# One encoder block on one core: bias rows copied with the repetitions outermost, and kept results loaded later in the down projection

## The chip, the cores and the metric

The kernel runs on 1 core of one Trainium2 chip, with every tensor in float32. The metric is the device time of one execution in microseconds (us), lower is better; several executions give a median.

## What is computed

One layer of a hybrid block over 512 positions of 1024 channels. The reference, cut to what matters here:

```python
def reference(...):
    h = _layernorm(x, ln_in_g, ln_in_b)
    mix = _mixing(h, ...)                      # SSD branch and attention branch, gated, one output projection
    h = _layernorm(DN_ALPHA * h + mix, ln1_g, ln1_b)
    f = _conv_ffn(h, ffn_w_up, ffn_conv_w, ffn_conv_b, ffn_w_down)
    return _layernorm(DN_ALPHA * h + f, ln2_g, ln2_b)

# attention, per block of 128 queries:
    logits = jnp.einsum('bthc,btkc->bthk', ql, kv)
    bias = jnp.take(rel_bias, _t5_bucket(idx - qpos[None, :, None]), axis=0)   # 16 heads, by key minus query
    logits = logits + bias.transpose(0, 1, 3, 2)

def _conv_ffn(h, w_up, conv_w, conv_b, w_down):
    u = _causal_dwconv(h @ w_up, conv_w, conv_b)
    a, v = jnp.split(u, 2, axis=-1)
    return (jax.nn.silu(a) * v) @ w_down       # w_down is 2816 x 1024
```

## The kernel before

**Products.** Each float32 operand is split into a high part (ACT copies it, L178 or L192) and a low part (DVE subtracts, L179 or L193), and TensorE (PE) adds three products, high by high, high by low and low by high, at L254. So every weight block passes through a DMA into `wraw` (issued by SyncE, SP), an ACT copy into `whi` and a DVE subtraction into `wlo` before PE may use it. There are four `wraw` buffers and three pairs `whi`, `wlo`. PE's order is fixed by hand (`chain`), and it runs through the program almost without a pause.

**The SSD stage** (to about 440 us) projects one block after another for four groups `g`. `in_x`, `in_b` and `in_c` end in a convolution (`conv_silu`: ACT at L649, three DVE steps at L652, ACT at L654, DVE at L655), `in_z` in a gate (ACT L688, DVE L689). `ssd_d` leaves two results in PSUM, which DVE (L813) and then POOL (L814, L824) turn into `v`, and ACT squares `v` (L830). `out_br` projects the results of the group before; for the first group ACT moves its sums from PSUM to `mssd` (L702), and only then is that PSUM buffer (`pacc`, three of them) free for the next projection. ACT, DVE and POOL each work strictly in their own order.

**The bias rows.** The bias depends on key minus query only, so each head has one row of 384 numbers (`UW`) in `rb_d`. `t5_copy(q)` writes 128 copies (`P`) of the rows of four heads into `rs_d`, from DRAM to DRAM, 768 KB in one DMA on SP's queue; it is called four times, q = 0 to 3, at fixed places of the SSD stage for groups 1 and 2. The attention stage reads `rs_d` with a row step of UW - 1 into one tile `toe` per head (L1017), which gives each query its shifted row.

**The up projection and what it keeps.** The down projection multiplies sums and differences of blocks, and takes pairs of up results (operands `fX`, made in `operands`). Six of the up results go to DRAM as `fo_d`, and one combination of each pair as `q_d` (`spill`, L1273, on POOL's queue). In the down projection (`NC` = 11 steps `c`, each 24 products long), they come back by `loaded` (L1537) into the tiles `f0` to `f5` and `f10` to `f14`, 256 KB each. `late(c + 4, ...)`, called for c = 4, 5 and 6, uses `f0` to `f5`; `q_split`, from c = 5 on, uses `f10` to `f14`. The weights of step c come by `w_sums(c)`: a half from `w_dq` and `sd_d` (L1491, L1492) and a second 512 KB from `sd_d` (L1493), into `raw` or `wraw`; in the lists below `raw_9797` and `raw_9798` are the two parts of c = 0.

**What sets the order.** `w_sums` issues at a high priority and each `loaded` behind the weight load written last (`issue_after(last_w)`), so SP's list is a mixture of both in the order in which the scheduler met them. SP's DMAs share one queue with at most eight in flight: each waits until the one eight places before it is done, and whatever SP waits for holds all that is behind it. ACT and DVE steps of the down projection are ordered by due times (`plan`).

Of the kernel before, what the change touches and what calls it, by code (L numbers as in the profile page):

```python
# [16 lines left out]
P = 128  # L17
# [14 lines left out]
UW = 384  # L32
# [42 lines left out]
def block_kernel(ctx, tc, A, out):  # L75
    nc = tc.nc
# [15 lines left out]
    def wt(tag, shape, name, dtype=F32):  # L92
        return wk.tile(shape, dtype, name=name, tag=tag, bufs=BUFS[tag])
# [18 lines left out]
    def acc_tile():  # L112
        return ps("acc", 3)
# [6 lines left out]
    def any_tile(tags):  # L120
        rot[0] += 1
        return ps(tags[rot[0] % len(tags)])
# [84 lines left out]
    def w_(name, s, **kw):  # L207
        return wload(A[name][s], **kw)
# [115 lines left out]
    rb_d = dram.tile([AH, UW], F32, name="rb_d")  # L324
    rs_d = dram.tile([AH, P, UW], F32, name="rs_d")
# [5 lines left out]
    fo_d = dram.tile([6, P, T], F32, name="fo_d")  # L331
# [178 lines left out]
    for j in range(2, 4):  # L510
        p = any_tile("abc")
# [367 lines left out]
    def t5_copy(q):  # L879

        n = AH // 4
        with tc.issue_after(last_w[0].ins):
            nc.sync.dma_start(rs_d[q * n:(q + 1) * n], bass.AP(tensor=rb_d.tensor, offset=rb_d.offset + q * n * UW,
                                                               ap=[[UW, n], [0, P], [1, UW]]))

    decays()
    latents()
# [51 lines left out]
    for g in (1, 2):  # L939
        run([in_x(g, 3), in_z(g, 0), in_z(g, 1), in_b(g + 1), out_br(g - 1, 0), out_br(g - 1, 1), out_br(g - 1, 2)],  # L940
            pair(g, 0, AT, root=AT[0], gm=(26, 29),
                 more=[(45, pin), *([(18, t5_load), (46, t5_rows)] if g == 1 else [(30, t5_copy, 2)])]))
        run([in_x(g + 1, 0), in_z(g, 2), in_c(g + 1), in_x(g + 1, 1), in_z(g, 3), out_br(g - 1, 3),
             in_x(g + 1, 2)], pair(g, 2, AT, [(12, ssd_b, g + 1), (38, ssd_cb, g + 1), *([(42, pin), (30, t5_copy, 3)] if g == 2 else [(12, t5_copy, 0), (44, t5_copy, 1)])]))
# [224 lines left out]
    for n in range(KD):  # L1169
        w, p = merges[n] if n < len(merges) else (w_("w_br_att", n), None)  # L1170
# [3 lines left out]
        p, first = (p, NP - 1) if p else (acc_tile(), 0)  # L1174
# [77 lines left out]
    def f_tile(c, dtype):  # L1252
        return fp.tile([P, T], dtype, name=f"f{c}", tag=f"f{c}")
# [181 lines left out]
    for s in range(3, 2 * KF + 1):  # L1435
# [16 lines left out]
        elif s < 2 * KF:  # L1452
            p = acc_tile() if s % 2 else any_tile("abc")
# [19 lines left out]
    def step(p, x_, i, w, first, last):  # L1473

        for j, (a, b) in enumerate(((0, 0), (1, 0), (0, 1))):
            mm(p, x_[a][:, tok(i)], w[b], start=first and j == 0, stop=last and j == 2)
# [6 lines left out]
    def w_sums(c, k0, k1):  # L1483

        with tc.high_priority(offset=400):
            if c % 4 < 2 and c < NC - 1:
                r = [wt("g4" if c % 4 else "k4", [P, D], "raw") for _ in range(2)]
            else:
                r = [wrw.tile([P, D], F32, name="wraw", tag="wraw") for _ in range(2)]
            with tc.issue_after(mark.ins):  # L1490
                nc.sync.dma_start(r[0][:, :T], A["w_dq"][c][:, 0])  # L1491
                nc.sync.dma_start(r[0][:, T:], sd_d[c][:, 0])  # L1492
                last_w[0] = nc.sync.dma_start(r[1].rearrange("p (a b) -> p a b", a=2), sd_d[c][:, 1:3])  # L1493
            if c % 3:
                d = [room[c % 3 - 1][:2], room[c % 3 - 1][2:]]
            else:
                d = [whl_pair() for _ in range(2)]
            for (hi, lo), src, k in zip(d, r, (k0, k1)):
                parts(k, k + 1.2, hi, lo, src)
        b11, t1, t3, t2 = [(hi[:, half_of(h)], lo[:, half_of(h)]) for hi, lo in d for h in range(2)]  # L1500
        return {"A11": b11, "S1": t1, "S3": t3, "S2": t2}
# [19 lines left out]
    lc, fO, fQ = [0], {}, {}  # L1521
# [11 lines left out]
    def loaded(c, src):  # L1533

        t = f_tile(c, F32)
        with tc.issue_after(last_w[0].ins):
            nc.sync.dma_start(t, src)  # L1537
        return t

    def late(c, k):  # L1540

        r0, r1 = fO[2 * c - 16], fO[2 * c - 15]
        s = wt("v", [P, T], "s")
        b, a = [(l_tile(), l_tile()) for _ in range(2)]
        z = l_tile()
        tt(k, s[:, L_], r0[:, R_], r1[:, R_], OP.subtract)
        tt(k, s[:, R_], s[:, L_], r0[:, L_], OP.subtract)
        tt(k, r0[:, R_], r0[:, L_], r0[:, R_], OP.subtract)
        parts(k + 1, k + 1.9, *b, s)
        parts(k + 1.6, k + 2.6, *a, r0)  # L1550
        parts(k + 2.2, k + 3.3, z[:, L_], z[:, R_], r1[:, R_])
        tt(k + 3.3, r1[:, R_], r1[:, L_], s[:, R_], OP.add)
        fX.append({"A11": [t[:, L_] for t in a], "S3": [t[:, R_] for t in a], "S1": [t[:, L_] for t in b],
                   "S2": [t[:, R_] for t in b], "A22": [z[:, L_], z[:, R_]]})
        fQ[c] = r1
# [7 lines left out]
    def q_split(c, k):  # L1563
        x_ = l_tile(), l_tile()
        parts(k, k + 0.8, *x_, fQ[c])
        qs.append(x_)
# [8 lines left out]
    def w_next():  # L1575
        n = wn[0]
        wn[0] += 1
        part = halves_[2 * n:2 * n + 2]
        srcs = [sd_d[c][:, 3] if kind == "X4" else A["w_dq"][c][:, 3 if kind == "B21" else 2] for kind, c in part]
        k = early.get(n, tB + use[n] * STEP - 6)  # L1580
        for key, w in zip(part, w_pair(srcs, k, cyc[n % 7])):
            wB[key] = w

    for c in range(NC):
        t = c * PAIR
        k0, k1 = {0: (-9.5, -4.6), 1: (0.2, 1.4), 2: (3.2, 4.6)}.get(c, (t - 5.5, t - 4.3))
        w = w_sums(c, k0, k1)
        if c in (1, 2):
            for j in range(3):
                fO[3 * c + j - 3] = loaded(3 * c + j - 3, fo_d[3 * c + j - 3])  # L1590
        for q, j in {1: ((0, 10), (1, 11)), 2: ((2, 12), (3, 13), (4, 14)), 6: ((5, 0), (6, 2)), 7: ((7, 4),)}.get(c, ()):
            fQ[q] = loaded(j, q_d[q])
        if c in (4, 5, 6):
            late(c + 4, t - 3)
        for q in {5: (0, 1), 6: (2, 3), 7: (4, 5), 8: (6, 7), 9: (8, 9)}.get(c, ()):
            q_split(q, t + 0.5 + 2.2 * (q % 2))
        if c == NC - 1:
            h1 = [wt("k4" if i < 2 else "g4", [P, D], "h1") for i in range(NT)]
            for i in range(NT):
                nc.sync.dma_start(h1[i], h1_d[:, i])  # L1600
            for _ in range(4):
                w_next()
        prods = [(U, "A11"), (P6, "S2"), (P7, "S3"), (P5, "S1")]
        for p, x_ in prods if c else (prods[0], prods[3], prods[2], prods[1]):
            for i in range(2):
                step(p[i], fX[c][x_], i, w[x_], c == 0, c == NC - 1)
# [104 lines left out]
    n = T // 2  # L1711
# [99 lines left out]
```

## Time and profile before

| | us |
|---|---|
| median of 3 runs | 1080.3 |
| lowest and highest run | 1078.89, 1081.57 |
| the profiled execution | 1078.5 |
| its span, first to last instruction | 1076.8 |
| PE busy | 1060.1 |
| DVE busy | 873.5 |
| ACT busy | 551.3 |
| POOL busy | 240.3 |

The span leaves 1.7 us of the profiled execution's time outside it. PE is busy for 98% of the span, and the other engines are busy less. So what matters is where PE is idle, how long, and what ended each of those idle times; an idle time of another engine matters only if PE waits for what it does next.

### The profile page before, as it was taken

What the parts mean: (1) busy time and instruction counts of PE and PEld (TensorE: products, weight loads), DVE (VectorE), ACT (ScalarE), POOL (GpSimd) and SP (SyncE); (2) the same over time, 40 slices, a digit from 0 to 9 for tenths busy, and PEclk for the clock granted to TensorE, in tenths of its full rate; (3) what the DMA queues carried; (4) which work ended last, traced back from release to release, by engine and by line L of the source; (5) the groups of instructions that cost most, each with busy time, mean ns of one, the idle gap of its engine ahead of it and who ended that gap; (6) DMA issues with size and microseconds to landing.
All of it is one profiled execution on the core that took longest, in us unless ns stands there. A gap on an engine that the chain in (4) does not pass through costs nothing.

```text
span 1076.8 us, 16632 instructions
## 1 busy us (share of the span) xinstructions
PE 1060.1 (98%) x5973; PEld 908.8 (84%) x5973; DVE 873.5 (81%) x1574; ACT 551.3 (51%) x968; POOL 240.3 (22%) x276
## 2 busy tenths in 40 slices
PE   8999999998999999999999999999999999999997
PEld 7888888887888888888777877889899999988886
DVE  8667787884899998448998976756979989989797
ACT  5444664553625544345555633405567767765631
POOL 4010214303141334104444444043000000000001
PEclk9999999999999999999999999999999999999999
DMA  7877688878887755687997763744466666777753
GB/s 288 292 186 217 187 185 184 230 177 270 220 245 222 149 160 132 162 303 191 246 216 147 177 199 132 230 122 89 136 185 206 189 203 198 256 276 258 225 186 120
DMA packets 82610, 215.24 MB, mean 200 GB/s; under 512 B 9280, under 2 KB 13936, under 8 KB 82352
## 3 DMA queue, kind: packets, MB, share of 16 engines
q1 hardware_dynamic: 69744, 182.20, 51.3%
q0 software_dynamic: 12784, 31.99, 19.6%
q8 instruction: 47, 0.77, 0.3%
q14 instruction: 35, 0.29, 0.1%
HBM read 201.93 MB, written 71.98 MB: 254 GB/s over the span
## 4 chain that ended last, share of the span: by engine, by line
PE 91%; issue 4%; DVE 2%; DMA 1%; ACT 1%; POOL 1%; DVEq 0%; POOLq 0%; ACTq 0%; SPq 0%
PE pacc L254 53%; PE ptr L1390 8%; PE pacc L1390 6%; PE ptr L254 6%; PE pc L254 5%; PE pb L254 2%; PE pa L254 2%; PE pacc L278 2%; PE ptr L278 1%; PE pa L257 1%; PE ptr L257 1%; PE pb L257 1%; DMA raw<-sd_d 1%; PE pa L278 1%; PE pc L278 1%
## 5 line engine op out<-in xcount | busy, mean ns | idle before, releaser
L254 PE MATMUL pacc<-hhi,whi 128*128 128x512 f32 (+1 forms) x536 | 217.2, 405 | 3.0 <-ACT mssd L702 2.2
L254 PE MATMUL pacc<-hlo,whi 128*128 128x512 f32 (+1 forms) x536 | 210.5, 393 | 0.5 <-DVE hlo L432 0.5
L254 PE MATMUL pacc<-hhi,wlo 128*128 128x512 f32 (+1 forms) x536 | 208.8, 391 | 0.1
L192 ACT ACTIVATE whi<-wraw 128x1024 fp32r<-128x1024 f32 x109 | 115.2, 1058 | 180.9 <-PE pacc L254 137.1
L193 DVE TENSOR_TENSOR wlo<-wraw,whi 128x1024 fp32r<-128x1024 f32 x109 | 142.9, 1311 | 61.4 <-ACT whi L192 57.7
L254 PEld LDWEIGHTS pacc<-hlo,whi 128*128 128x128 f32 (+1 forms) x536 | 100.8, 188 | 23.7 <-DVE hlo L432 1.8
L254 PEld LDWEIGHTS pacc<-hhi,whi 128*128 128x128 f32 (+1 forms) x536 | 101.2, 189 | 22.7 <-ACT mssd L702 2.6
L254 PEld LDWEIGHTS pacc<-hhi,wlo 128*128 128x128 f32 (+1 forms) x536 | 101.2, 189 | 18.3 <-DVE wlo L394 0.4
L178 ACT ACTIVATE whi<-wraw 128x1024 fp32r<-128x1024 f32 (+1 forms) x64 | 60.8, 949 | 49.4 <-PE ptr L1390 21.3
L179 DVE TENSOR_TENSOR wlo<-wraw,whi 128x1024 fp32r<-128x1024 f32 (+1 forms) x64 | 69.7, 1088 | 15.4 <-ACT whi L178 14.9
L1029 POOL TENSOR_TENSOR tm<-mask,toe 128x128 f32<-128x128 f32 (+1 forms) x64 | 44.7, 703 | 105.1 <-DVE mn L1046 86.4
L652 DVE SCALAR_TENSOR_TENSOR cv<-pacc,cwb,cv 128x511 f32<-128x511 f32 (+2 forms) x72 | 53.2, 740 | 0.3
L1049 ACT ACTIVATE l<-l,mn 128x128 f32<-128x128 f32 (+1 forms) x64 | 35.7, 559 | 30.8 <-DVE mn L1046 29.4
L254 PE MATMUL pacc<-yhi,whi 128*128 128x512 f32 x128 | 50.3, 395 | 0.0
L254 PE MATMUL pacc<-ylo,whi 128*128 128x512 f32 x128 | 49.8, 389 | 0.0
L254 PE MATMUL pacc<-yhi,wlo 128*128 128x512 f32 x128 | 49.8, 389 | 0.0
L212 POOL DMA_DIRECT2D su_d<-su_d x32 | 27.1, 890 | 84.5 <-DVE wlo L193 39.7
L814 POOL TENSOR_TENSOR v<-v,eaB 128x384 f32<-128x384 f32 x16 | 18.0, 1136 | 105.5 <-DVE v L813 87.1
L763 ACT ACTIVATE G<-G,acT 128x128 f32<-128x128 f32 x128 | 40.1, 392 | 0.0
L174 POOL TENSOR_TENSOR rs_y<-rs_v,mhalf 128x4 f32<-128x4 f32 (+1 forms) x10 | 10.5, 1055 | 131.3 <-DVE rs_v L172 131.3
L1273 POOL DMA_DIRECT2D q_d<-fs x8 | 4.5, 558 | 150.5 <-DVE fs L1308 150.5
L1390 PE MATMUL ptr<-h1lo,whi 128*128 128x256 f32 x128 | 36.2, 283 | 0.0
(649 smaller groups left out, 2924.8 us busy)
## 6 DMA issues: line engine op xcount, KB each, us to landing
su_d<-in_w_up_dram SPq DMA_DIRECT2D x32, 512.0 KB, 8.7
wraw<-su_d SPq DMA_DIRECT2D x64, 256.0 KB, 3.6
wraw<-in_w_xbc_dram SPq DMA_DIRECT2D x24, 512.0 KB, 7.7
wraw<-in_w_up_dram SPq DMA_DIRECT2D x48, 256.0 KB, 2.8
G<-ac_d SPq DMA_DIRECT2D x16, 512.0 KB, 6.3
wraw<-in_w_z_dram SPq DMA_DIRECT2D x16, 512.0 KB, 4.5
su_d<-in_w_up_dram POOLq DMA_DIRECT2D x16, 512.0 KB, 10.7
su_d<-su_d POOLq DMA_DIRECT2D x32, 256.0 KB, 8.2
```

What stands on the lines that cost most here:

```text
L178: nc.scalar.activation(hi, src, AF.Copy)
L179: return nc.vector.tensor_tensor(lo, src, hi.bitcast(F32), OP.subtract)
L192: nc.scalar.activation(hi[:, :cols], raw[:, :cols], AF.Copy)
L193: last_lo[0] = nc.vector.tensor_tensor(lo[:, :cols], raw[:, :cols], hi[:, :cols].bitcast(F32), OP.subtract)
L254: pe(nc.tensor.matmul(p, a, b, start=start, stop=stop).ins)
L257: pe(nc.tensor.transpose(p, a, b).ins)
L278: nc.tensor.matmul(p, x[a][:, tok(i)], w[b][h], start=first and j == 0, stop=last and j == 2)
L652: nc.vector.scalar_tensor_tensor(y[:, d:], p[:, :T - d], cwb[:, 24 * k + c:24 * k + c + 1], y[:, d:], OP.mult, OP.add)
L763: i = nc.scalar.activation(G[:, h, c], G[:, h, c], AF.Relu, bias=acT[:, c, q:q + 1], scale=-1.0)
L1029: last_pow[0] = nc.gpsimd.tensor_tensor(tm[:, :K - f], maskt[i][:, f:], self.toe[:, 2 * P - K + f:], OP.add)
L1049: nc.scalar.activation(l[:, :K], l[:, :K], AF.Exp, bias=self.mn[:, ic], scale=-1.0, accum_out=self.sm[:, ic])
L1390: pe(nc.tensor.matmul(p, w[x_][:, tok(k)], r[k][y_], start=first and k + j == 0, stop=last and k == 3 and j == 2, skip_group_check=True).ins)
```

## The change

It has two parts, and touches two places.

The first part is the copy of the bias rows. The same 512 rows of 1536 bytes move from `rb_d` to `rs_d` and end at the same addresses, but the DMA is described with the 128 repetitions as its first dimension and the four heads as its second, on both sides. The second part is where `loaded` is called: `f0` to `f2` at c = 3 in place of 1, `f3` to `f5` at c = 4 in place of 2, `f10` and `f11` at 2 in place of 1, `f12` and `f13` at 4 and `f14` at 5 in place of 2.

```diff
@@ t5_copy
         with tc.issue_after(last_w[0].ins):
-            nc.sync.dma_start(rs_d[q * n:(q + 1) * n], bass.AP(tensor=rb_d.tensor, offset=rb_d.offset + q * n * UW,
-                                                               ap=[[UW, n], [0, P], [1, UW]]))
+            nc.sync.dma_start(rs_d[q * n:(q + 1) * n].rearrange("h p u -> p h u"),
+                              bass.AP(tensor=rb_d.tensor, offset=rb_d.offset + q * n * UW,
+                                      ap=[[0, P], [UW, n], [1, UW]]))
@@ the loop over c of the down projection
-        if c in (1, 2):
+        if c in (3, 4):
             for j in range(3):
-                fO[3 * c + j - 3] = loaded(3 * c + j - 3, fo_d[3 * c + j - 3])
-        for q, j in {1: ((0, 10), (1, 11)), 2: ((2, 12), (3, 13), (4, 14)), 6: ((5, 0), (6, 2)), 7: ((7, 4),)}.get(c, ()):
+                fO[3 * c + j - 9] = loaded(3 * c + j - 9, fo_d[3 * c + j - 9])
+        for q, j in {2: ((0, 10), (1, 11)), 4: ((2, 12), (3, 13)), 5: ((4, 14),), 6: ((5, 0), (6, 2)), 7: ((7, 4),)}.get(c, ()):
```

On SP, in the SSD stage around the first two copies, the order stays and the form of the copy differs; the numbers behind a DMA are its dimensions:

```order
 L877 DMA rb_d<-rf 16x384
-L883 DMA rs_d<-rb_d 512x1x384
-L186 DMA wraw<-in_w_br_ssd_dram 128x1024
-L883 DMA rs_d<-rb_d 512x1x384
+L883 DMA rs_d<-rb_d 128x4x384
+L186 DMA wraw<-in_w_br_ssd_dram 128x1024
+L883 DMA rs_d<-rb_d 128x4x384
 L186 DMA wraw<-in_w_xbc_dram 128x1024
```

What moved: nothing; both copies keep their places ahead of a weight load each.

On SP at the turn from the up to the down projection, before the change (`f0` to `f14` are the tiles of the kept results, `raw_9798` is the second part of the weights of c = 0, `wraw_9923` of c = 3):

```order
L1537 DMA f0_9843<-fo_d_122 128x512
L1537 DMA f1_9845<-fo_d_122 128x512
L1537 DMA f2_9847<-fo_d_122 128x512
L1537 DMA f10_9849<-q_d_121 128x512
L1537 DMA f11_9851<-q_d_121 128x512
L1537 DMA f3_9886<-fo_d_122 128x512
L1493 DMA wraw_9923<-sd_d_119 128x1024
L1537 DMA f4_9888<-fo_d_122 128x512
L1537 DMA f12_9892<-q_d_121 128x512
L1537 DMA f13_9894<-q_d_121 128x512
L1537 DMA f14_9896<-q_d_121 128x512
L1493 DMA raw_9798<-sd_d_119 128x1024
```

And the same place after it (the line numbers are one higher, `wraw_9905` is the second part of c = 3, `raw_9947` and `raw_9948` are c = 4):

```order
L1538 DMA f10_9876<-q_d_121 128x512
L1538 DMA f11_9878<-q_d_121 128x512
L1494 DMA wraw_9905<-sd_d_119 128x1024
L1538 DMA f0_9917<-fo_d_122 128x512
L1538 DMA f1_9919<-fo_d_122 128x512
L1538 DMA f2_9921<-fo_d_122 128x512
L1494 DMA raw_9798<-sd_d_119 128x1024
L1492 DMA raw_9947<-in_w_dq_dram 128x512
L1493 DMA raw_9947<-sd_d_119 128x512
L1494 DMA raw_9948<-sd_d_119 128x1024
L1538 DMA f3_9956<-fo_d_122 128x512
L1538 DMA f4_9958<-fo_d_122 128x512
```

What moved: ahead of `raw_9798` there are five kept results in place of ten; `f3`, `f4`, `f5`, `f12` and `f13` stand behind the weights of c = 4, and `f14` behind those of c = 5. The lists of PE and POOL are the same as before; on ACT and DVE the same steps stand in the same order.

## Rows read from the trace of the kernel before

**Rows 1.** Busy time of the engines in stretches of 25 us from the span's start (length, then busy time and count of PE, its weight load, DVE, ACT and POOL, the granted PE clock, the mean busy share of the 16 DMA engines, and GB/s).

```profile
225.00:250.00 25.00, 24.16 (x145) 20.48 (x143) 15.68 (x32) 13.29 (x29) 1.64 (x2) 1.00 0.84 236
250.00:275.00 25.00, 21.82 (x100) 18.01 (x101) 14.90 (x22) 7.35 (x11) 10.69 (x10) 0.93 0.85 242
...
375.00:400.00 25.00, 25.00 (x145) 21.05 (x144) 25.00 (x40) 10.48 (x16) 8.19 (x8) 1.00 0.59 168
...
950.00:975.00 25.00, 24.22 (x108) 19.73 (x107) 20.33 (x26) 14.09 (x18) 0.54 (x1) 1.00 0.80 274
```

**Rows 2.** The timeline of PE from 248 to 265 us (start, length, engine, line, operation, count, and in brackets the idle time before it and what ended that).

```profile
248.12 1.04 PE L254 MATMUL ptr<-G,xd 128*64 128x128 f32 x16
251.02 1.13 PE L254 MATMUL ptr<-bc 128*128 128x128 f32 x8 [1.86 <-DVE bc L655]
...
260.48 0.79 PE L254 MATMUL pacc<-hhi,whi 128*128 128x512 f32 x1 [2.16 <-ACT mssd L702]
...
263.91 0.39 PE L254 MATMUL pacc<-hlo,whi 128*128 128x512 f32 x1
264.14 0.39 PE L254 MATMUL pacc<-hhi,whi 128*128 128x512 f32 x1
```

**Rows 3.** The timelines of ACT from 236 to 262 us and of DVE from 248 to 254 us.

```profile
247.30 1.06 ACT L192 ACTIVATE whi<-wraw 128x1024 fp32r<-128x1024 f32 x1 [9.12 <-PE pb L254]
...
258.83 0.63 ACT L830 ACTIVATE sq<-v 128x512 f32<-128x512 f32 x1 [4.83 <-POOL v L824]
...
259.84 0.59 ACT L702 ACTIVATE mssd<-pacc 128x512 f32<-128x512 f32 x1
...
248.39 1.23 DVE L193 TENSOR_TENSOR wlo<-wraw,whi 128x1024 fp32r<-128x1024 f32 x1 [6.71 <-ACT whi L192]
...
253.76 0.74 DVE L813 SCALAR_TENSOR_TENSOR v<-xs,Dv,pc 128x512 f32<-128x512 f32 x1
```

**Rows 4.** SP's own timeline over the first two copies; the length of a DMA_DIRECT2D is the time that SP spent on issuing it.

```profile
213.62 0.74 SPq L883 DMA_DIRECT2D rs_d<-rb_d  x1
214.47 9.84 SPq L186 DMA_DIRECT2D wraw<-in_w_br_ssd_dram  x1
224.36 0.67 SPq L883 DMA_DIRECT2D rs_d<-rb_d  x1
225.13 11.03 SPq L186 DMA_DIRECT2D wraw<-in_w_xbc_dram  x1
```

**Rows 5.** DMA issues with their size and the time from issue to landing: first the two weight loads of rows 4, then the medians over the whole run of loads from the second tensor, of the copies from DRAM to DRAM by which SP brings weights of the up projection into `su_d` (first dimension 128), and of the loads `G`, which read two DRAM rows 128 times over.

```profile
wraw<-in_w_br_ssd_dram SPq DMA_DIRECT2D x1, 512.0 KB, 21.2
wraw<-in_w_xbc_dram SPq DMA_DIRECT2D x1, 512.0 KB, 22.1
...
su_d<-in_w_up_dram SPq DMA_DIRECT2D x32, 512.0 KB, 8.7
...
wraw<-in_w_xbc_dram SPq DMA_DIRECT2D x24, 512.0 KB, 7.7
G<-ac_d SPq DMA_DIRECT2D x16, 512.0 KB, 6.3
```

**Rows 6.** Stretches in which, by SP's timeline, little but the rest of a bias copy was under way (copies of 224.36, 250.02 and 295.87), and one of full load.

```profile
230.50:235.50 5.00, 5.00 (x24) 4.14 (x23) 2.46 (x6) 5.00 (x11) 0.00 (x0) 1.00 0.30 87
254.50:258.00 3.50, 3.50 (x17) 2.81 (x15) 2.79 (x4) 0.00 (x0) 3.42 (x3) 1.00 0.26 103
300.00:303.50 3.50, 3.50 (x33) 2.91 (x28) 3.27 (x8) 1.06 (x1) 2.39 (x3) 1.00 0.32 106
...
249.20:251.00 1.80, 0.00 (x0) 0.01 (x1) 1.80 (x4) 0.34 (x1) 0.00 (x0) 1.00 1.05 414
```

**Rows 7.** SP's timeline from 948 to 966 us.

```profile
948.77 1.30 SPq L1537 DMA_DIRECT2D f<-fo_d  x3
...
955.25 0.32 SPq L1493 DMA_DIRECT2D raw<-sd_d  x1
```

**Rows 8.** DMA issues with time to landing: that load of 955.25, and the same kind issued at 965.46.

```profile
raw<-sd_d SPq DMA_DIRECT2D x1, 512.0 KB, 7.8
...
raw<-sd_d SPq DMA_DIRECT2D x1, 512.0 KB, 3.5
```

**Rows 9.** Timelines of ACT, DVE and PE behind it, from 958 to 972 us.

```profile
963.12 1.06 ACT L1289 ACTIVATE whi<-raw 128x1024 fp32r<-128x1024 f32 x1 [4.12 <-DMA raw<-sd_d]
...
964.60 0.76 ACT L1325 ACTIVATE u<-pacc,pvec 128x512 f32<-128x512 f32 x1
965.26 1.99 ACT L1289 ACTIVATE h1hi<-raw 128x1024 fp32r<-128x1024 f32 x2
...
967.49 1.53 DVE L1330 SCALAR_TENSOR_TENSOR u<-pacc,pvec,u 128x511 f32<-128x511 f32 x2
...
963.46 0.62 PE L254 MATMUL ptr<-whi,fw 128*128 128x512 f32 x2
...
969.16 0.70 PE L254 MATMUL pacc<-whi,fw 128*128 128x512 f32 x2 [0.78 <-ACT h1lo L1289]
```

**Rows 10.** The first uses of kept results in the down projection, on DVE: `late` at c = 4, 5 and 6.

```profile
979.41 0.42 DVE L1292 TENSOR_TENSOR s<-f,f 128x256 f32<-128x256 f32 x1
...
986.34 0.42 DVE L1292 TENSOR_TENSOR s<-f,f 128x256 f32<-128x256 f32 x1
...
992.80 0.42 DVE L1292 TENSOR_TENSOR s<-f,f 128x256 f32<-128x256 f32 x1
```

## The prediction

> **What bounds the kernel now.** I read the stretches of 25 us first, then the timeline of each engine where PE was not full. PE is full nearly everywhere; the three stretches of [rows 1] with a gap are 225 to 275 us, where 4.02 us are missing and the granted clock falls to 0.93, and 950 to 975, where 0.78 is missing. The span's first and last stretches aside, PE's other gaps are small. The timeline of PE shows the first place as two idle times, 1.86 us before 251.02 and 2.16 us before 260.48, and after the second one a stretch of long matmuls [rows 2]: from 260.48 to 263.91 nine matmuls start, in 3.43 us, while a normal step is 0.23 us (263.91 to 264.14), nine of them 2.07; so 1.36 us more are lost to the clock.
>
> **Why PE waits there.** Follow the first gap back. PE waited for DVE's last convolution step (L655), DVE for ACT, and ACT sat idle for 9.12 us before the weight copy of 247.30 [rows 3]. The view names PE's `pb` as releaser, but the weight load which that copy reads was issued at 225.13 [rows 4] and took 22.1 us to land [rows 5]: 247.23, just ahead of 247.30. I take the load as the cause. A load of that tensor takes 7.7 us in the median. The second gap has the same root: the `mssd` copy that PE waits for stands in ACT's order behind a square of `v`, this waits for POOL, POOL for DVE's `v`, and DVE is behind by what it could not do before 248 [rows 3].
>
> **Why that load took 22 us.** It and the load before it stand right behind a bias copy each, and SP spent 9.84 and 11.03 us on merely issuing them, where it spends 0.7 on a copy [rows 4]: the queue took no more. In three stretches where little but a copy is left, the DMA engines are busy to 0.26 to 0.32 and move 87 to 106 GB/s; in a full stretch they are busy to 1.05 and move 414 [rows 6]. A quarter of 16 engines is four, as many as the copy's first dimension has heads. So a copy runs on four engines, and takes 786 KB / 103 GB/s = 7.6 us with nothing beside it, more with the queue of POOL beside it. Every weight load has a share on those four, and is done only when they are.
>
> **Part one, the copy.** The bytes and the 512 rows stay; SP's order stays. What changes is that the first dimension has 128 entries, like every weight load. If the copy then runs on 16 engines at the rate of one engine in [rows 6], it takes 7.6 / 4 = 1.9 us. That is the lower bound of its time; the upper is 7.6, on all engines, if reading the same four rows is what limits it. I take 1.9, by the two nearest rows: the copies into `su_d` go from DRAM to DRAM with 128 first, and land in 8.7 us, and `G` reads two rows 128 times over, and lands in 6.3, where a weight load takes 7.7 [rows 5]. Both copies and both loads are then 2.6 MB, 6.3 us at 414 GB/s; POOL's additions beside them may double that. Issued at 225 as before, the load would land at 233 (median 7.7) to 240 (double). How late may it be? From the start of ACT's weight copy to the end of the step that PE waits for first it is 251.02 - 247.30 = 3.7 us, and PE is there at 249.16; so ACT must start by 245.4. For the second gap it is 260.48 - 247.30 = 13.2 us at most, and PE comes to that place at 258.32 - 1.86 = 256.5; so by 243.3. The load is ahead of both. DVE stood idle for 6.71 us before 248.39 [rows 3] and can then do that work earlier, so the first `v` follows PE's own results (up to 249.2 [rows 2]) near 248.4 in place of 253.76. From there to the end of `mssd` it was 260.4 - 253.8 = 6.7 us, so `mssd` is ready near 255.1, 1.4 us before PE needs it.
>
> Both gaps go, and the long matmuls with them, since nothing is left that starves PE: 1.86 + 2.16 + 1.36 = 5.4 us. The bounds are 0 (the load still late) and 5.5 (a few long matmuls after the first gap too). Nothing is next in line: SP is free some 20 us sooner, and the copies at 250 and 296 delay loads for which PE did not wait. The work behind keeps its distance to PE, since ACT, DVE and POOL had been waiting there too, and start earlier by as much.
>
> Here a page has something to say against one term. The Trainium skill ("TensorE: Matmul & The Clock Gate", Part 1) has the clock fall to half after about one idle window of 3.4 us; by that rule an idle time of 2.16 us would not have caused the long matmuls, the 1.36 us might stay, and the sum of both parts would be 4.8 in place of 6.2. The rows have a gap of 2.16 us and the long matmuls right behind it, so I keep the term.
>
> **Part two, the loads.** PE's gap before 969.16 is named after an ACT step, but the PSUM buffer it waits for is read last by DVE's convolution step of 967.49, which ends at 969.02 [rows 9]. That one follows ACT's `h1hi`, and ACT had waited 4.12 us for the second part of the weights of c = 0. This load was issued at 955.25 and took 7.8 us [rows 7, 8], behind ten kept results and one weight load issued from 948.77 on, 3.1 MB; now five of the ten stand there. 1.3 MB less at the 414 GB/s of [rows 6] is 3.2 us: it lands in 4.6 us, between 3.5 (the same kind with an idle queue [rows 8]) and 7.8 (no effect). SP can't issue it earlier, it waits for its buffer. ACT's copy starts at 959.9, but `u` from the last up product can't start before PE ends that product (its next one begins at 963.46), so `h1hi` starts near 964.4 in place of 965.26, and DVE's step ends 0.9 earlier, at 968.1, where PE needs it at 969.16 - 0.78 = 968.4 [rows 9]. The gap of 0.78 us goes; bounds 0 and 0.9. The delayed loads are issued by about 966 and the first of them are needed at 979.41, 986.34 and 992.80 [rows 10]; `f0` to `f2` still come near 953. That cover is over 13 us, so this costs nothing.
>
> **The sum.** 5.4 + 0.8 = 6.2 us. Against the profiled execution's own 1078.5 us (span 1076.8 and 1.7 around it) that gives 1072.3. The median is 1.8 us above that execution, and 1080.3 - 6.2 = 1074.1.
>
> **The rivals.**
> (a) *The second gap stays.* Its chain runs through POOL and ACT, whose work takes 13.2 us in the trace; my 1.4 us of slack rests on DVE catching up. If POOL's `v` comes as it did, only 1.86 + 0.78 are gained: 1077.7, or 1076.3 if the clock holds. Against it: DVE's idle 6.71 us before 248.39.
> (b) *The copy does not spread*, because the four heads still decide. Then part two alone counts: 1079.5. The trace has no repeating copy from DRAM to DRAM with 128 first, which leaves it open; that a 512 KB copy into `su_d` lands in 8.7 us speaks against it, since on four engines at 103 GB/s it would need 5.1 with nothing beside it and, as the loads of [rows 4] show, far more in traffic. The Trainium skill ("DMA: Bandwidth & Descriptors", "Why a DMA increments its semaphore by 16 and not by 1") takes the number of engines from the first dimension of both sides that isn't 1, the largest divisor of both up to 16; by that rule this rival has no chance, and the quarter share agrees with 4 before.
> (c) *Given back later.* DVE is full from 375 to 400 [rows 1]. If it can't follow an earlier PE, PE waits there, and 5.4 us are lost again: 1079.5. Against it: PE does not wait for DVE there now, and DVE's work arrives as much earlier as PE.
> (d) *Slower.* Sixteen engines reading the same four rows block each other. At 100 GB/s in total a copy takes 7.6 us on every engine, and loads behind it land as late as now, so the time stays. It decides above 7.6 us: at 12 us the two copies push the load of 225.13 back by another 2 x 4.4 us, ACT and PE wait that much longer, and the time is 1080.3 + 8.8 - 0.8 = 1088.3. `G` speaks against it [rows 5].
>
> **How the numbers follow.** The forecast, both parts as worked out, has 0.68; (a) 0.12, (b) 0.06, (c) 0.10, (d) 0.04. About what a measurement of this kernel can tell from no change is 0.3%, 3.2 us: faster means below 1077.1. That holds for the forecast and a third of (a): 0.72. (b), (c) and the rest of (a) are within: 0.24. Slower 0.04. The range takes the forecast with the 1.5 us by which runs differ, and (a): 1072.5 to 1077.8, with (b), (c) and (d) outside.
>
> **What would show it.** In the profile after: a share of DMA time near 1 during the copies and no stretch at a quarter; SP's weight loads behind the copies issued in under 1 us, landing in under 14; no ACT idle time of 9 us near 240; PE without gaps and a clock of 1.00 from 225 to 275; the second weight part of c = 0 landing in about 4.6 us, and no gap of PE behind it. I am wrong if the copy still shows a quarter share, if ACT still waits for that load, or if new gaps of PE appear behind 300 us.

## The result

The changed kernel takes 1071.68 us (median of 6 runs, 1071.60 to 1072.22); beside it the kernel before took 1079.6 us (6 runs, 1078.48 to 1082.89). The ratio is 0.9923, 95% interval [0.9907, 0.9938]: faster by 7.9 us. I had said 1074.1, with a range from 1072.5 to 1077.8: the sign and the places are right, the gain is 1.7 us larger than forecast, and the time lies 0.8 us below the range. The profiled execution took 1071.71 us, with a span of 1070.0; so between the two profiled executions it is 6.8 us.

The same 25 us stretches of the kernel after as in [rows 1], and at the end the whole start of the down projection (length, busy time and count of PE, its weight load, DVE, ACT, POOL, granted clock, DMA share, GB/s):

```profile
225.00:250.00 25.00, 25.00 (x152) 21.38 (x151) 21.11 (x40) 13.94 (x30) 2.35 (x3) 1.00 1.02 316
250.00:275.00 25.00, 25.00 (x129) 21.17 (x128) 14.96 (x21) 10.75 (x18) 11.75 (x12) 1.00 0.97 217
375.00:400.00 25.00, 25.00 (x151) 21.28 (x150) 24.97 (x49) 10.03 (x25) 10.04 (x9) 1.00 0.72 175
950.00:975.00 25.00, 25.00 (x112) 20.50 (x111) 21.12 (x28) 14.35 (x19) 1.08 (x2) 1.00 0.82 280
...
950.00:1000.00 50.00, 50.00 (x222) 41.21 (x221) 43.31 (x61) 31.73 (x45) 1.08 (x2) 1.00 0.78 264
```

PE is full in all of them and the granted clock is 1.00: the 4.02 us of 225 to 275 are back, the half-speed stretch with them, and so are the 0.78 us near 968. DVE is as full from 375 to 400 as before and PE does not wait for it.

SP's timeline after, over the same copies and loads as [rows 4], and below it the issues from 213 to 222 us with their time to landing [rows 5]:

```profile
214.00 0.59 SPq L883 DMA_DIRECT2D rs_d<-rb_d  x1
214.68 1.10 SPq L186 DMA_DIRECT2D wraw<-in_w_br_ssd_dram  x1
215.83 1.59 SPq L883 DMA_DIRECT2D rs_d<-rb_d  x1
219.09 0.33 SPq L186 DMA_DIRECT2D wraw<-in_w_xbc_dram  x1
```

```profile
rs_d<-rb_d SPq DMA_DIRECT2D x2, 768.0 KB, 18.7
...
su_d<-su_d POOLq DMA_DIRECT2D x2, 256.0 KB, 13.3
wraw<-in_w_br_ssd_dram SPq DMA_DIRECT2D x1, 512.0 KB, 19.2
wraw<-in_w_xbc_dram SPq DMA_DIRECT2D x1, 512.0 KB, 18.6
```

SP spends 1.10 and 0.33 us on the two loads in place of 9.84 and 11.03, and comes to the second one 6 us sooner. It lands at 219.09 + 18.6 = 237.7, where it landed at 247.2. The time to landing itself is hardly shorter, and a copy too is under way for 18.7 us: copies, loads and POOL's additions now fill all engines together (share 1.02 from 225 to 250 us). What has changed is that nothing waits behind four of the engines while twelve stand idle. The engines of a copy can be counted in the trace, which also holds the events by which a DMA reports that a part of it has landed. A weight load has 16 of them. The first copy of the kernel before had four, at 230.0 to 234.4 us, besides one that came 1.1 us after its issue began; each copy of the kernel after has 16.

ACT and PE after, in the places of [rows 2, 3 and 9] (start, length, engine, line, operation, and in brackets the idle time before it and what ended that):

```profile
241.24 1.06 ACT L192 ACTIVATE whi<-wraw 128x1024 fp32r<-128x1024 f32 x1 [3.02 <-PE pacc L254]
...
253.76 0.60 ACT L702 ACTIVATE mssd<-pacc 128x512 f32<-128x512 f32 x1
...
953.96 1.06 ACT L1290 ACTIVATE whi<-raw 128x1024 fp32r<-128x1024 f32 x1 [0.82 <-DMA raw<-sd_d]
```

```profile
249.12 1.16 PE L254 MATMUL ptr<-bc 128*128 128x128 f32 x8
...
293.29 1.09 PE L254 MATMUL pc<-G,xd 128*64 128x128 f32 x16
...
957.60 0.62 PE L254 MATMUL ptr<-whi,fw 128*128 128x512 f32 x2
...
962.37 0.70 PE L254 MATMUL pacc<-whi,fw 128*128 128x512 f32 x2
```

ACT's weight copy starts at 241.24 and waits for PE, no longer for the load (3.02 us in place of 9.12). No row of PE has a bracket. Steps of the same name tell what each part brought: the first one of the down projection moved from 963.46 to 957.60 (5.86 us, part one), the one with the old gap from 969.16 to 962.37 (6.79, so 0.93 for part two).

### The profile page after: what moved, and what is told of

It is laid out like the page before. It is cut to its first block, busy times and chain, and to the rows that moved or that the text cites. A ratio compares the mean times of both kernels' runs of the same rounds, so it can differ in the third digit from the quotient of the medians.

```text
span 1070.0 us, 16636 instructions
## 1 busy us (share of the span) xinstructions
PE 1058.8 (99%) x5973; PEld 908.5 (85%) x5973; DVE 873.2 (82%) x1574; ACT 552.1 (52%) x968; POOL 240.2 (22%) x276
## 4 chain that ended last, share of the span: by engine, by line
PE 97%; DMA 1%; DVE 1%; ACT 0%; issue 0%; POOL 0%; DVEq 0%
PE pacc L254 58%; PE ptr L1391 9%; PE ptr L254 7%; PE pacc L1391 6%; PE pc L254 5%; PE pb L254 3%; PE pa L254 2%; PE pacc L278 2%; PE ptr L278 1%; PE pa L257 1%; PE ptr L257 1%; PE pb L257 1%; DMA htok_d<-x 1%; PE pa L278 1%; PE pc L278 1%; PE pb L278 1%
## 5 line engine op out<-in xcount | busy, mean ns | idle before, releaser
L1391 PE MATMUL ptr<-h1hi,wlo 128*128 128x256 f32 x128 | 36.2, 283 | 0.0
```

What stands on the lines that cost most here:

```text
L1391: pe(nc.tensor.matmul(p, w[x_][:, tok(k)], r[k][y_], start=first and k + j == 0, stop=last and k == 3 and j == 2, skip_group_check=True).ins)
```

## The experiments

The theory: a copy runs on as many DMA engines as the largest divisor up to 16 of its first dimension; on four, two copies delay one weight load, PE waits for it, and the clock falls behind the wait. The rivals: the order of the rows does it, not the engine count; any copy on few engines would do. And one question more: the kernel before spreads over 4.4 us in six runs, the one after over 0.6. I had carried over, as a constant, that the median of before lies 1.8 us above its profiled execution.

**The copy alone** (`e1_copy_only`): the first hunk of the change.

> The copy with its 128 repetitions first; the loads of the down projection stand as before. Theory: the copies alone bring 5.9 us between two profiled executions (the start of the down projection moved from 963.46 to 957.60), so the span is near 1071 with gaps of PE at 249 and 258 gone and the clock at 1.00 there, and PE's gap of 0.8 us behind c = 0 of the down projection is back. If the spread of the kernel before (1078.5 to 1082.9 in six runs) comes from the work behind the copies too, the runs lie within 1 us of each other, at a median near 1072.6. Rival on the spread: it has nothing to do with the copies; then the runs here spread over 3 us or more, and the median is near 1073.7.

1073.17 us (1072.74 to 1074.04, 6 runs) against 1079.39 (23 runs, 1077.75 to 1083.44); ratio 0.994 [0.9926, 0.9954]. No gap at 249 or 258, clock 1.00, and the gap behind c = 0 is there with 0.70 us. The spread is 1.3 us, a little more than the 1 us expected, and the median lies 0.6 us above the 1072.6 expected; but it was 5.7 us in the kernel before beside it, and the rival had asked for 3 or more. So most of the spread goes with the copies.

**The loads alone** (`e2_loads_only`): the second hunk.

> The copy as before, heads first; the kept results of the down projection are loaded later. Theory: 0.9 us less than before, median near 1078.7, both PE gaps at 249 and 258 and the long matmuls still there, and the spread of the runs as wide as before (3 us or more). Rival on the spread: it comes from the loads of the down projection; then the runs lie within 1 us of each other, near 1077.7.

1078.51 us (1076.16 to 1081.89, 12 runs), ratio 0.9987 [0.9973, 1.0]: 0.88 us less than before, where 0.9 was expected, but not clear of noise. The spread is 5.7 us, so it doesn't come from these loads. The profiled execution shows what varies. ACT and PE near 250 us:

```profile
249.71 1.06 ACT L192 ACTIVATE whi<-wraw 128x1024 fp32r<-128x1024 f32 x1 [11.49 <-DMA wraw<-in_w_xbc_dram]
```

```profile
253.43 2.05 PE L254 MATMUL ptr<-bc 128*128 128x128 f32 x8 [4.23 <-DVE bc L655]
```

Here the view names the load as ACT's releaser, where it named PE's `pb` in [rows 3]. There is one gap of 4.23 us in place of two of 1.86 and 2.16.

**Order or engines** (`e3_rows_124_4`, `e4_rows_112_16`): the new order of the rows, with each copy cut in two.

```diff
-            nc.sync.dma_start(rs_d[q * n:(q + 1) * n], bass.AP(..., ap=[[UW, n], [0, P], [1, UW]]))
+            for r0, r1 in ((0, 124), (124, P)):        # e4: 112 in place of 124
+                nc.sync.dma_start(rs_d[q * n:(q + 1) * n, r0:r1].rearrange("h p u -> p h u"),
+                                  bass.AP(..., ap=[[0, r1 - r0], [UW, n], [1, UW]]))
```

> The order of after (repetitions first), the loads as before, and each copy cut in two: 124 repetitions, then 4. Of 124 the largest divisor up to 16 is 4, and of 4 it is 4. Theory, that the number of engines decides, which is the largest divisor of the first dimension up to 16: a copy is back on four engines, SP takes some 10 us to issue the weight load behind it, its landing is above 20 us, both PE gaps return, and the time is as before, 1078 to 1082. Rival, that the order of the rows (four heads side by side, and so which rows are written together) decides, or that any first dimension with many entries spreads: as the kernel with the copy alone, near 1072.6.

> The same cut in two, at 112 repetitions and 16; both have 16 as largest divisor up to 16. Theory: as the kernel with the copy alone, 1072 to 1073.5, no gap at 249 and 258. If the cut in two itself costs something (two more waits and issues on SP for each copy), it shows here: above 1074.

124 and 4: 1078.55 us (1076.90 to 1082.09, 12 runs), ratio 0.999 [0.9978, 1.0002]. 112 and 16: 1073.5 us (1072.78 to 1073.69, 6 runs), ratio 0.9941 [0.9927, 0.9954]. The same order of rows, the same number of DMAs, a first dimension of 124 or 112: 5 us. SP's timeline and PE's gaps with 124 and 4:

```profile
214.68 9.37 SPq L186 DMA_DIRECT2D wraw<-in_w_br_ssd_dram  x1
224.10 11.99 SPq L884 DMA_DIRECT2D rs_d<-rb_d  x3
236.19 0.38 SPq L186 DMA_DIRECT2D wraw<-in_w_xbc_dram  x1
```

```profile
252.23 2.04 PE L254 MATMUL ptr<-bc 128*128 128x128 f32 x8 [3.12 <-DVE bc L655]
...
261.70 0.50 PE L254 MATMUL pacc<-hhi,whi 128*128 128x512 f32 x1 [0.75 <-ACT mssd L702]
```

SP is held as before, and both gaps are back. SP is now blocked in one of the three issues of bias rows ahead of the load (the 4 rows of the first copy, then 124 and 4 of the second), and the load lands in 12.2 us, not in over 20 as I had put it; but it is issued 11 us later, and lands at 248.4. The landing events say the same: four for each piece of 124 or of 4 (and the early one), 16 for each piece of 112 or of 16. The order is out as a cause; the divisor is what counts. This is the rule by which the Trainium skill ("DMA: Bandwidth & Descriptors", "Why a DMA increments its semaphore by 16 and not by 1") gives the number of engines, and the runs agree with it.

**Fewer and more engines** (`e7_rows_119_9`, `e8_rows_122_6`): the same cut at 119 and at 122.

> Repetitions first, cut in 119 and 9; the largest divisors up to 16 are 7 and 9. Loads as before. Theory, by bytes for the engine that has most: four engines 196 KB of a copy each, and the load lands at 247.2; sixteen 49 KB, and it lands at 237.7; seven 112 KB, on the line between them 241.8, ahead of the 243.3 from which PE waits. So no gap: 1073 to 1074.5, like the copy on 16 engines, and a narrow spread. Rival: anything under 16 engines clogs the queue; then gaps as before and 1077 or more.

> Repetitions first, cut in 122 and 6; the largest divisors up to 16 are 2 and 6. Loads as before. Theory, on the same line: two engines 393 KB each, and the load lands near 260, some 15 us after PE wants it; one long gap of PE of 12 to 18 us, and a low clock of two or three steps of 3.4 us behind it: 1086 to 1094. Rival: the number of engines isn't what counts; then 1073 to 1083 like the others.

119 and 9: 1073.77 us (1072.93 to 1074.01), ratio 0.9938 [0.9921, 0.9955]. 122 and 6: 1105.96 us (1102.98 to 1107.33), ratio 1.0236 [1.0212, 1.0259]. Counted by their landing events the pieces run on 7, 9, 2 and 6 engines. The issues of the load, first with 119 and 9, then with 122 and 6 (issued at 232.94 and 251.95), and with 122 and 6 what PE does. The last line is a stretch in which little but the third copy was under way (length, busy time and count of PE, granted clock, DMA share, GB/s): the share of 0.13 is two of 16 engines.

```profile
wraw<-in_w_xbc_dram SPq DMA_DIRECT2D x1, 512.0 KB, 8.7
```

```profile
wraw<-in_w_xbc_dram SPq DMA_DIRECT2D x1, 512.0 KB, 9.0
```

```profile
264.75 2.04 PE L254 MATMUL ptr<-bc 128*128 128x128 f32 x8 [15.56 <-DVE bc L655]
...
309.21 0.80 PE L254 MATMUL pacc<-yhi,whi 128*128 128x512 f32 x1 [3.85 <-DVE zs L689]
```

```profile
268.00:274.00 6.00, 6.00 (x24) 0.83 0.13 51
```

It lands at 232.94 + 8.7 = 241.6 and at 251.95 + 9.0 = 260.95; the line through the bytes for one engine had said 241.8 and near 260. That it fits so closely is in part luck: the line goes through one execution of the kernel before, and in three others, shown below, the load came 2.3 to 5.5 us later. That fewer engines land later holds for all of them. With seven engines the load is still ahead of 243.3 and there is no gap, though SP was held for 16.41 us, where it was 11.03 in the kernel before. With two, the gap of 15.56 us is in the forecast of 12 to 18, but the time is 12 us above the upper end of mine. I had counted only the first two copies: the later ones, which on four engines cost nothing, now delay loads as well. A load `G` issued behind the third copy, at 278.97, lands 21.14 us later; ACT waits 8.06 us for it and PE 3.85 us, before 309.21. In all, 24.7 us are lost by the step that stands at 293.29 in the kernel after and at 317.95 here. The profiled execution (1103.01) is 29.8 us above 1073.2, the median of the copy alone, and the first step of the down projection stands 29.76 us behind that of the kernel after (987.36 and 957.60). So the other 5 us are lost in between, among them a gap of 1.91 us before 358.11 with 3.4 us of half clock behind it, and one of 0.46 before 375.93; the rest is not taken apart.

**One copy out of the way** (`e6_copy1_later`): heads first, on four engines, but the second copy stands further back on SP's queue.

```diff
-... [(42, pin), (30, t5_copy, 3)] if g == 2 else [(12, t5_copy, 0), (44, t5_copy, 1)]
+... [(42, pin), (30, t5_copy, 3), (44, t5_copy, 1)] if g == 2 else [(12, t5_copy, 0)]
```

> Heads first, on four engines, as before, and the loads as before; but the second of the two copies that stand near 214 and 224 is moved later on SP's queue, behind the loads of this stretch, to where the third copy stood. Theory: the delay is two copies on the same four engines ahead of one weight load; with one copy less, the load that landed at 247.2 lands by 238 to 241, ahead of the 243.3 from which PE waits, though SP is still held for some 10 us by the first copy. Both gaps go, the clock stays at 1.00, and the time is that of the copy on 16 engines, 1073 to 1074.5, with a spread under 2 us. Rival 1: any four-engine copy in this stretch is enough; then the gaps stay, 1077 or more. Rival 2: the moved copy starves another load near 250 to 300; then a new gap of PE shows there.

1073.64 us (1072.65 to 1074.45), ratio 0.9939 [0.9922, 0.9956]. SP's timeline and the load's issue:

```profile
214.08 0.74 SPq L883 DMA_DIRECT2D rs_d<-rb_d  x1
214.92 10.71 SPq L186 DMA_DIRECT2D wraw<-in_w_br_ssd_dram  x1
225.73 0.41 SPq L186 DMA_DIRECT2D wraw<-in_w_xbc_dram  x1
```

```profile
wraw<-in_w_xbc_dram SPq DMA_DIRECT2D x1, 512.0 KB, 14.3
```

The load lands at 240.0 and no gap of PE stands from 225 to 330. So the gaps come neither from four engines alone nor from SP being held (10.71 us here), but from two such copies ahead of one load; with one of them it lands 3.3 us before the 243.3 from which PE waits.

**Both parts once more** (`e5_both_again`): the changed kernel.

> The changed kernel once more, beside others, to size part two and the spread. Theory: part two is worth what stands between the kernel with the copy alone (median 1073.17) and this one; by the PE instructions of the two profiles it is 0.8 us (from the start of the down projection to its last matmuls 104.85 with the copy alone, 104.03 with both), so this kernel is at 1071.7 to 1072.4, and its runs lie within 1.3 us, since the copies run on 16 engines. Rival: the loads bring more than the gap of 0.7 us (the medians are 1.5 apart); then it is at 1071.7 again and the part of it that the gap does not cover must show in other places of the profile.

1072.01 us (1071.67 to 1072.53), beside 1080.56 of before on that chip (11 runs, 1077.55 to 1083.41); ratio 0.9924 [0.9907, 0.9941]. From the start of the down projection to its last matmuls it is 104.03 us in both profiles with part two, and 104.85, 104.84, 104.76 and 105.08 in those of the four kernels with part one (or its like) alone. By this part two is worth 0.73 to 1.05 us; by the medians of these four kernels, less this run's 1072.01, it is 1.2 to 1.8. Where the rest of that comes from stays open.

**Where the spread comes from** (`e9_before_1`, `e9_before_2`, `e9_before_3`): the kernel before, one execution each.

> The kernel before, unchanged, profiled once more. Theory of the spread: ACT's copy of the late weight load starts when the load lands, and PE's step behind it starts 3.72 us later (247.30 and 251.02 before, 249.71 and 253.43 with the loads alone, 248.51 and 252.23 with 124 and 4). So the first gap is ACT's start less 245.4; the second gap comes on top; and each step of 3.4 us at half clock costs some 1.5 us. The time of an execution is then 1073.3 (median of the kernel with the copy alone) + first gap + second gap + 1.5 for each such step, within 0.9 us. Rival: the spread arises elsewhere; then executions with the same gaps differ by more than that, or the missing time shows as gaps in another place.

> The same a second time: 1073.3 + both gaps of PE near 250 and 260 + 1.5 for each step of 3.4 us at half clock, within 0.9 us. An execution near 1082 or 1083 would have to show a load that lands past 250, or two gaps with two or three such steps.

> The same a third time: 1073.3 + both gaps of PE near 250 and 260 + 1.5 for each step of 3.4 us at half clock, within 0.9 us.

PE near 250 us in the first, the second and the third:

```profile
253.35 2.05 PE L254 MATMUL ptr<-bc 128*128 128x128 f32 x8 [4.17 <-DVE bc L655]
```

```profile
254.12 2.05 PE L254 MATMUL ptr<-bc 128*128 128x128 f32 x8 [5.00 <-DVE bc L655]
```

```profile
256.47 2.05 PE L254 MATMUL ptr<-bc 128*128 128x128 f32 x8 [7.29 <-DVE bc L655]
...
265.96 0.50 PE L254 MATMUL pacc<-hhi,whi 128*128 128x512 f32 x1 [0.55 <-ACT mssd L702]
```

All profiles in which the load is late, in order of ACT's weight copy; the lag is how far PE's step `pc<-G,xd` of 293.29 stands behind that of the kernel after:

| profile | ACT's copy | gaps of PE, us | half clock, us | lag, us | time, us |
|---|---|---|---|---|---|
| before | 247.30 | 1.86, 2.16 | 3.4 | 5.85 | 1078.5 |
| 124 and 4 | 248.51 | 3.12, 0.75 | 3.4 | 5.56 | 1079.66 |
| before, first | 249.64 | 4.17 | 6.8 | 6.75 | 1078.86 |
| loads alone | 249.71 | 4.23 | 6.8 | 7.11 | 1078.91 |
| before, second | 250.40 | 5.00 | 6.8 | 7.63 | 1081.12 |
| before, third | 252.75 | 7.29, 0.55 | 6.8 | 9.82 | 1082.02 |

PE's step starts 3.71 or 3.72 us after ACT's copy in every row, as expected. My sums from the gaps and 1.5 us for each step of low clock give 1080.5, 1081.3 and 1084.1: right for the second, too long by 1.6 and 2.1 for the others. The lag, which holds gaps and clock without a sum, shows where the error lies. It is 0.4 us shorter than gaps and price of the clock in the first (6.75 against 7.17) and 1.0 in the third (9.82 against 10.84): part of the low time falls into the gap itself, where it costs nothing. The other 1.2 and 1.1 us lie outside this stretch, where I had put the constant 1073.3: time less lag is 1072.1 and 1072.2. In the four executions of the kernel before, the lag varies by 4.0 us and the time by 3.5, while time less lag varies by 1.4 (1072.1 to 1073.5), about as much as the runs of the copy alone. So most of the spread is made in this stretch, by when the load lands; the rest elsewhere, for instance in the gap behind c = 0, which was 0.18 to 1.27 us long in the profiles without part two. What makes the load land at 247 or at 253 with the same instructions ahead of it stays open.

## Where the prediction was right, and the step that failed

*The bound, and why PE waits.* Right. The load behind the copies was the cause of both gaps, named in later profiles by the view itself; the load was late because of two copies on four engines ahead of it (one alone does not do it, as the moved copy shows).

*The copy spreads to 16 engines.* Right, and (b) and (d) are out. The shorter times to landing were not: I expected the loads to land in under 14 us, and it was 18.6 and 19.2. The load is issued at 219.09, not at the 225 that I had kept, and its landing at 237.7 is inside my 233 to 240: there two misses cancelled, which is luck. No run shows a copy that takes 1.9 us; the shortest time to landing of one in the kernel after is 7.3 us (the fourth, issued at 290.02).

*Both gaps go.* Right; rival (a) is out. `mssd` starts at 253.76 and ends at 254.4, where I had it ready at 255.1. (c) is out as well: 375 to 400 is as full, and the gain of 5.85 us at 293 is still 5.86 at 957.60.

*The size, 1.86 + 2.16 + 1.36 = 5.4.* It was 5.85. Set PE's steps side by side: behind the first gap they are 1.88 apart, with the second it is 4.20, and at 263.91, which was 258.09 after, 5.82. So the second gap was worth 2.32 (the profile models the end of the matmul ahead of it), and the low clock 1.62 in place of 1.36: I had counted nine matmuls from 260.48 to 263.91, and there are eight.

*Part two, 0.8.* 0.93. The second weight part lands in 5.2 us (4.6 forecast) and is issued 0.7 us sooner against PE (8.87 us ahead of the first step of the down projection in place of 8.21), which I had ruled out; ACT's copy of it starts at 953.96, 3.6 us ahead of that step, where it was 0.3 ahead. The delayed loads cost nothing: PE is full to 1000.

*The step that failed: "the median is 1.8 us above that execution, and 1080.3 - 6.2 = 1074.1".* I took the way from the profiled execution to the median as a constant of the measurement and gave it to the kernel after as well. It was part of what the change removes. The profiled execution of before had the load land earliest of the six in the table, with a lag of 5.85 us; the three later ones of the same kernel had 6.75, 7.63 and 9.82. With the stall gone, the runs of the kernel after lie within 0.6 us, and its median (1071.68) is that of its profiled execution (1071.71) to 0.03 us. Of the 2.4 us between 1074.1 and 1071.68 this step is 1.8; the other 0.6 are the two terms above, 5.85 and 0.93 in place of 5.4 and 0.8. Three runs from 1078.89 to 1081.57 were enough to see that the spread (2.7 us) was nearly half as large as the gain, and the range, which gave 1.5 us to the difference of runs, should have gone down to what is left when the spread goes too: 1078.5 - 6.2 = 1072.3, and less by what the gaps cost more in a median execution than in this one.

## What to carry over

Look at the first dimension of every DMA, copies from DRAM to DRAM too: with 128 or 112 the copy used all engines, with 124 it was back on a quarter of them, and two such copies delayed a load behind them by 9.5 to 15 us. When a stall is to be removed, ask whether it is as long in each run: if runs of the kernel spread and those of its neighbours don't, the spread belongs to the stall and goes with it, and the profiled execution is only one draw of it. Check where a late transfer turns into a wait: the load could be 3.9 us later than with 16 engines at no cost (seven engines), and what it was late by beyond 245.4 was paid by PE in full, with the clock on top.

## What the runs showed of the hardware

The low clock comes in pieces of 3.4 us. PE's stretches of 3.4 us around it, of the kernel with 124 and 4, and of the first later execution of the kernel before (length, busy time and count of PE, granted clock, DMA share, GB/s):

```profile
248.40:251.80 3.40, 0.71 (x14) 1.00 0.97 386
251.80:255.20 3.40, 2.97 (x11) 0.50 0.72 228
255.20:258.60 3.40, 3.40 (x16) 1.00 0.26 103
```

```profile
248.30:251.70 3.40, 0.88 (x18) 1.00 1.01 389
251.70:255.10 3.40, 1.75 (x9) 0.51 0.82 286
255.10:258.50 3.40, 3.40 (x10) 0.50 0.28 108
258.50:261.90 3.40, 3.40 (x16) 0.99 0.52 117
```

The kernel before, in two pieces around its gap of 1.86 us and in the one of the gap of 2.16 us:

```profile
246.66:250.07 3.41, 2.50 (x38) 1.00 1.03 402
250.07:253.48 3.41, 2.46 (x15) 1.00 0.86 339
...
256.90:260.31 3.41, 1.42 (x7) 1.00 0.68 180
```

After a gap of 3.12 us the clock is at 0.50 for one piece, after 4.17 for two: the piece in which PE is busy for 1.75 of 3.40 us is followed by another low one, the piece with 2.97 by full speed. The pieces lie on a grid of their own: in all thirteen traces the changes of the granted clock stand a whole number of 3.413 us apart (in the kernel before 256.00 us, 75 pieces, lie between 4.31 and the fall at 260.31). What decides, by these traces, is how long PE is busy in one piece, not the length of a gap by itself. The gap of 1.86 us lies across an edge, PE is busy for 2.50 and 2.46 us in the two pieces, and the clock stays at 1.00; nearly all of the gap of 2.16 us lies in one piece, PE is busy for 1.42 us in it, and the next is low. Cut at the grid, the thirteen traces agree (some 4000 pieces, from the first full speed on, with PE's busy time as the profile models it). At full clock a piece with PE busy for 1.50 us or less is followed by a low one, and one with 1.57 us or more is not; at half clock a piece with 2.58 us or less is followed by another low one, and one with 3 us or more by full speed. So one and the same stall costs one piece or two by where on the grid PE starts again. The length is that of the window in the Trainium skill ("TensorE: Matmul & The Clock Gate", Part 1), and the runs agree on it; that a whole window must be idle they don't bear out, a gap of 2.16 us was enough. I expected none of this.

Nor had I expected how long SP can be held without harm. With 119 and 9 its timeline has, for three issues of bias rows together (9 of the first copy, 119 and 9 of the second),

```profile
216.42 16.41 SPq L884 DMA_DIRECT2D rs_d<-rb_d  x3
```

and yet the load issued behind it at 232.94 landed in 8.7 us: the time was spent in waiting to issue rather than in waiting to land.
